# Attention's values as one group of 1,024 columns behind the gated heads, and GLA begun two column groups sooner

## The chip, the cores and the metric

The kernel runs on one core of a Trainium2 chip. The metric is the device time of one launch in microseconds. Each engine takes its instructions in order: TensorE (PE, with its weight loads apart as PEld), VectorE (DVE), ScalarE (ACT), GpSimd (POOL) and SyncE (SP), whose queue issues most of the DMA transfers. Engines wait for one another by semaphores.

## The reference

One layer of a decoder: an RMS norm, one projection to nine groups of columns, differential softmax attention (8 heads) and gated linear attention (GLA, 4 heads) side by side on the same input, both gated, and an output projection with a norm and a residual.

```python
def hybrid_layer(x, layer_idx, pre_g, post_g, w_in, w_gk_up, b_gk,
                 lq1, lk1, lq2, lk2, subln_g, gla_g, w_out):
    h = rms_norm(x, pre_g)
    z = jnp.einsum('bsd,de->bse', h, w_in)
    qa, ka, va, ga, qb, kb, vb, gb, gk_low = split_columns(z)
    lam = exp(sum(lq1 * lk1)) - exp(sum(lq2 * lk2)) + lam_init
    # softmax(q1 k1^T) v - lam softmax(q2 k2^T) v, causal, per head of 128 columns of va
    oa = diff_attention(qa, ka, va, lam)
    oa = rms_norm(oa, subln_g) * (1.0 - lam_init)
    oa = oa * silu(ga)
    log_a = log_sigmoid(gk_low @ w_gk_up + b_gk) / 16.0
    # S_t = diag(exp(log_a_t)) S_{t-1} + k_t^T v_t ; o_t = q_t S_t, in chunks
    ob = gla_chunked(qb, kb, vb, log_a)
    ob = rms_norm(ob, gla_g) * silu(gb)
    y = jnp.einsum('bse,ed->bsd', concatenate([oa, ob], -1), w_out)
    return x + rms_norm(y, post_g)
```

S and D_MODEL are 1024; va, the values of attention, has 1,024 columns (8 heads of 128). All is fp32.

## The kernel before

**Number format.** Each fp32 factor is split in a high part, cast by ACT, and a low part, its difference, taken by DVE; a product is three matmuls (high·high, high·low, low·high).

**Products.** The projection h·w_in is done for column groups, called pairs here (`pairs`, L168): VB, KA, QA, QB, KB, GB, VA, GA, each group 256 columns. For every group the 2x2 block product of h (rows in two halves, inner dimension in two halves) is made by seven products instead of eight, with sums of blocks; `LEFT` (L320) says which sum of h's blocks a product n = 1..7 takes. (VA0,5) is product 5 of the values' group that begins at head 0. b11, b12, b21, b22 are the blocks of the weights: the first digit is the half of the rows, the second the half of the columns. Products 1 and 2 take single blocks, 5, 6 and 7 differences that DVE makes in place in the loaded tiles, and their results are summed from banks of PSUM: a bank of 512 columns named x, y or z; s, s1, s2 and s3 are copies of partial sums that ACT makes.

**Two shapes.** For all groups but VA and VB the weights (128x128) are the stationary factor and 512 rows of h move; a product is 12 matmuls of 128x512. VA and VB need the result with rows on partitions, so a block of h is stationary and 256 columns of weights move: two groups of 256 columns go together ("wide"), they share the weights of a product, and each product of a group is 24 matmuls of 128x256. VA is done as two such couples, VA0 with VA2 and VA4 with VA6, one for each half of the heads: 28 products.

**The order.** The list `order` holds the products, (group, n), one after the other; product 3 of a group is placed behind product 2 (or 5, 6) of the next one. `go` (L598) runs down that list: it prepares weights four products ahead (`prepare`, then `make_weights`: load, subtract, cast, low part), calls `step` for the product and then, through `fill`, one section of GLA. A scheduler keeps the order of the matmuls and sets that of the other engines' instructions. Weights of a product go through a ring of five tiles of 128x1024 (`NRING`, tag "ring"), loaded weights through four tiles of 512 KB (tag "raw").

**GLA beside it.** `gla` (L771 and following) is cut into sections by `yield`: 11 sections a half, 8 halves, 88 sections. A half loads its inputs, does pa and pk, the kv states, gpo (its output, copied by ACT to the tile go), the squares, gms (their sum by a matmul), and then norms and gates go, splits it, and stores high parts (from the tile gg) and low parts (from go) to mixe. Its tiles are those that attention will need later, one buffer each in the pool kp: q0, k0, q1, k1, ks0, ks1; go is in ks0; gan, the squares sqs and their split sq_hl, which the gms matmuls read, share k1. GLA begins when the order stands at (12, 5), the group GB2, and its 88 sections, one a product, end beside the gated heads, at GA6.

**What comes around.** `decay` (L682 and following) makes the decays of GLA heads, which the taking of QB and KB needs; `wo_step` prepares pieces of the output's weights. `take_values` (L396) adds two banks into c, splits it, and stores it in v_d, from where attention loads it. Attention itself follows the last products, those of KA6 and QA6.

Of the kernel before, what the change touches and what calls it, by code (L numbers as in the profile page):

```python
# [14 lines left out]
P = 128  # L15
# [4 lines left out]
HB = 4  # L20
# [11 lines left out]
def hymba_kernel(  # L32
# [58 lines left out]
    v_d = [tc.dram_tile([2, P, NT, P], F32, name=f"v{h}_d") for h in range(DA_HEADS)]  # L91
# [78 lines left out]
    pairs += [("KA", 0, KA), ("QA", 0, QA), ("QB", 0, QB), ("KB", 0, KB)]  # L170
    pairs += [("GB", g, GB + 256 * g) for g in range(2)]
    pairs += [("QB", 2, QB + 256), ("KB", 2, KB + 256)]
    pairs += [("GB", g, GB + 256 * g) for g in range(2, 4)]
    for h in (0, 4):
        pairs += [("VA", h, VA + h * P), ("VA", h + 2, VA + h * P + 256)]
        pairs += [(n, h + 2, c + h * P + 256) for n, c in (("KA", KA), ("QA", QA)) if not h]
        pairs += [(n, 4, c + 512) for n, c in (("KA", KA), ("QA", QA)) if h]
    pairs += [("GA", g, GA + g * P) for g in range(0, DA_HEADS, 2)]
    pairs += [("KA", 6, KA + 768), ("QA", 6, QA + 768)]

    def wide(p):
        return pairs[p][0] in ("VA", "VB")
# [3 lines left out]
    def load_raw(p, halves=(0, 1)):  # L186
        if p >= len(pairs):
            return
        c0 = pairs[p][2]
        for kh in halves:  # L190
            if kh not in raws.setdefault(p, {}):
                r = ap.tile([P, HB, 256], F32, tag="raw", name="w_raw", bufs=4)
                rows = slice(kh * 512, kh * 512 + 512)
                sp.dma_start(r, w_in[0, rows, c0 : c0 + 256].rearrange("(k p) c -> p k c", p=P))
                raws[p][kh] = r

    EARLY = 5
# [4 lines left out]
    for p in range(y):  # L204
        if wide(p) and p % 2:
            groups[-1].append(p)
        else:
            groups.append([p])
    for prev, group in zip([[]] + groups, groups):
        for n in (1, 2, 5, 6, 4, 7):  # L210
            if (group[0], n) not in order[:n_early]:
                order += [(p, n) for p in group]

            if n == (7 - len(group) if group[0] < EARLY else 2):
                order += [(p, 3) for p in prev]
# [4 lines left out]
    order += [(y, 1), (y, 2), (y - 1, 3), (y, 5), (z, 1), (z, 2), (z, 5), (y, 6), (z, 6), (y, 4)]  # L220
# [29 lines left out]
    def fetch_raw(p, n, i):  # L250

        if not wide(p):
            load_raw(p)
            if i >= n_early:
                load_raw(p + 1)
        elif p >= 4 or p == 0:
            load_raw(p)
            if p and n == 1:
                load_raw(p + 1)

            if n == 4:
                load_raw(p + 2, (0,))
                if p == 0:
                    load_raw(3, (0,))
            elif n == 7:
                if p == 0:
                    load_raw(3, (1,))
                else:
                    load_raw(p + 2, (1,))
        else:  # L270
            if n == 5:
                load_raw(2, (1,))
            elif n == 4:
                load_raw(4, (0,))
            elif n == 7:
                load_raw(4, (1,))

    def make_weights(i):
        p, n = order[i]
        if wide(p) and p % 2:  # L280
            ws[i] = ws_wide[p - 1, n]
            return
# [63 lines left out]

    decs = {}
# [48 lines left out]
    def take_values(p, half, unit, p0, p1):  # L396

        kind, n, _ = pairs[p - p % 2]
        tiles = slice(half * 4 + p % 2 * 2, half * 4 + p % 2 * 2 + 2)
        p0, p1 = (t.rearrange("p (n u c) -> p u n c", u=2, c=P) for t in (p0, p1))  # L400
        if kind == "VB":
            st = t_st("gv_st").rearrange("p (u n c) -> p u n c", u=2, c=P)
            dve.tensor_tensor(st, p0, p1, ALU.add)
            for u in range(2):
                sp.dma_start(gv_d[n + unit][u, :, tiles, :], st[:, u])
        else:
            c, hi = t_c("c"), t_st("v_hi", F32R)
            c, hi, lo = (
                t.rearrange("p (u n c) -> p u n c", u=2, c=P) for t in (c, hi, c.bitcast(F32R))
            )  # L410
            dve.tensor_tensor(c, p0, p1, ALU.add)
            act.copy(hi, c)
            dve.tensor_tensor(lo, c, fp(hi), ALU.subtract)
            for t, src in enumerate((hi, lo)):
                for u in range(2):
                    sp.dma_start(v_d[n + 2 * unit + u][t, :, tiles, :], fp(src[:, u]))

    sums = {}

    def step(i):  # L420

        p, n = order[i]
        kind, m, _ = pairs[p]
# [175 lines left out]
    def go(n):  # L599
        for _ in range(n):  # L600
# [137 lines left out]
    go(order.index((8, 2)) - made[0])  # L738
    go(2)
    decay(2)  # L740
    go(7)
# [148 lines left out]
    go(order.index((12, 5)) - made[0])  # L890
# [99 lines left out]
    def load_v(h):  # L990
        v = [smp.tile([P, NT, P], F32R, tag="v", name=f"v{t}", bufs=4) for t in range(2)]
        for t in range(2):

            with tc.issue_after(qk_load[0]) if h else nullcontext():
                ins = sp.dma_start(fp(v[t]), v_d[h][t])
# [535 lines left out]
```

## Time and profile before

| what | us |
|---|---|
| time, three runs | 978.72, 978.31, 978.85 (median 978.72) |
| the profiled execution's own time | 978.49 |
| its span | 976.7 |
| PE busy | 956.6 |
| DVE busy | 735.4 |
| ACT busy | 602.1 |
| products of VA in the trace | from 308.8 on |
| last gms matmuls of GLA | 569.7 |

The profile is of one execution. Its span is the time in which the engines' instructions lie, and the difference to the execution's own time lies before and behind them. A row of a group of instructions gives the line, the engine, the operation, the output and input tiles and their shape, then how many there are, their busy time and the mean of one in ns, and the idle time ahead of them with what ended it. A row of the timeline gives the start, the duration and the count of instructions run together. Since PE's matmuls are pipelined, the duration of a group reaches into the next; the distance from start to start is what a group takes of PE's time.

### The profile page before, as it was taken

Reading aid. Unit: us, or ns where it says so; the run is one execution under the profiler, and the core shown is the slowest. Engines: PE = TensorE matmul, PEld = TensorE weight load, DVE = VectorE, ACT = ScalarE, POOL = GpSimd, SP = SyncE. Lnnn points to the kernel's source line nnn. Section 1 sums busy time; section 2 is a strip of 40 time slices with the busy share of each in tenths; the row PEclk is TensorE's granted clock in tenths of the full one; section 3 lists DMA queues with packets and bytes.
Section 4 is the critical chain, followed back from the end, with each engine's and each line's share of the span. In section 5 each row is a group of like instructions: output and inputs, shape, how many; then the busy total and the mean of one; then the engine's idle time right before and its main releaser. Section 6 shows DMA issues by size and latency. Waiting matters only on the chain.

```text
span 976.7 us, 15689 instructions
## 1 busy us (share of the span) xinstructions
PE 956.6 (98%) x5282; PEld 828.3 (85%) x5282; DVE 735.4 (75%) x1452; ACT 602.1 (62%) x1164; POOL 193.8 (20%) x253
## 2 busy tenths in 40 slices
PE   6999999999999999999999999999999999999997
PEld 5998988888889998999888888878888888888785
DVE  6887597798775668676786776487888888898554
ACT  8642455487357446545566765366776687787773
POOL 4300000111121111100321102121322222443321
PEclk9999999999999999999999999999999999999999
DMA  9442446656675859986988766987747769994777
GB/s 355 142 117 86 138 136 204 227 177 236 229 258 166 269 164 328 285 266 205 285 283 251 250 194 199 395 267 271 220 147 238 245 199 366 323 296 105 151 208 149
DMA packets 146513, 220.45 MB, mean 226 GB/s; under 512 B 17104, under 2 KB 83664, under 8 KB 146336
## 3 DMA queue, kind: packets, MB, share of 16 engines
q1 hardware_dynamic: 132496, 178.80, 57.5%
q0 software_dynamic: 13936, 40.64, 14.2%
q8 instruction: 42, 0.69, 0.3%
q14 instruction: 39, 0.32, 0.1%
HBM read 133.93 MB, written 88.60 MB: 228 GB/s over the span
## 4 chain that ended last, share of the span: by engine, by line
PE 93%; DVE 3%; ACT 2%; DMA 1%; issue 1%; POOL 0%; DVEq 0%; SPq 0%; ACTq 0%; POOLq 0%
PE x L117 23%; PE y L117 15%; PE z L117 15%; PE ypart L117 13%; PE sc L117 7%; PE po L117 5%; PE yps L117 4%; PE wtr L120 3%; PE gpo L117 3%; PE kv L117 1%; PE gkl_ps L117 1%; PE pa L117 1%; DMA v_d<-c 1%; PE xT L120 0%; ACT junk L491 0%
## 5 line engine op out<-in xcount | busy, mean ns | idle before, releaser
L315 ACT CAST w<-w_raw 128x512 fp32r<-128x512 f32 (+1 forms) x164 | 112.3, 688 | 107.2 <-PE y L117 50.0
L316 DVE TENSOR_TENSOR w<-w_raw,w 128x512 fp32r<-128x512 f32 (+1 forms) x164 | 126.6, 773 | 57.0 <-ACT w L315 48.8
L1054 ACT ACTIVATE p<-p,stt 128x896 f32<-128x896 f32 (+7 forms) x128 | 99.3, 777 | 36.2 <-DVE stt L1044 33.1
L427 ACT COPY s<-x 128x512 f32<-128x512 f32 x84 | 49.0, 583 | 91.9 <-PE x L117 91.5
L296 DVE TENSOR_TENSOR w_raw<-w_raw 128x512 f32<-128x512 f32 (+1 forms) x96 | 75.8, 790 | 21.2 <-DMA w_raw<-in_w_in_dram 19.7
L588 POOL DMA_DIRECT2D wo_d<-wo_hi x32 | 17.6, 550 | 349.7 <-ACT wo_hi L584 349.7
L1044 DVE CUSTOM_DVE_ANT_0 p<-sc,maskt 128x512 f32<-128x512 f32 (+3 forms) x128 | 74.3, 585 | 15.6 <-PE sc L117 14.3
L1060 POOL TENSOR_SCALAR p<-p,stt,lam 128x1024 f32<-128x1024 f32 (+3 forms) x64 | 56.2, 879 | 146.0 <-DVE stt L1059 144.3
L117 PE MATMUL y<-h_hi,w 128*128 128x512 f32 x320 | 79.9, 392 | 0.0
L117 PE MATMUL x<-s_hi,w 128*128 128x512 f32 x320 | 79.8, 391 | 0.0
L117 PE MATMUL ypart<-wo_hi,m_hi 128*128 128x512 f32 x192 | 79.6, 414 | 0.1
L117 PE MATMUL z<-s_hi,w 128*128 128x512 f32 x320 | 79.6, 391 | 0.0
L117 PE MATMUL ypart<-wo_hi,m_lo 128*128 128x512 f32 x192 | 75.5, 393 | 0.0
L117 PE MATMUL ypart<-wo_lo,m_hi 128*128 128x512 f32 x192 | 75.4, 393 | 0.0
L117 PEld LDWEIGHTS x<-s_hi,w 128*128 128x128 f32 x320 | 59.8, 188 | 12.3
L117 PEld LDWEIGHTS y<-h_hi,w 128*128 128x128 f32 x320 | 59.8, 188 | 12.3
L117 PE MATMUL sc<-k,q 128*128 128x512 f32 (+1 forms) x192 | 69.0, 363 | 1.2 <-DVE stt L1044 1.2
L117 PEld LDWEIGHTS z<-s_hi,w 128*128 128x128 f32 x320 | 59.5, 188 | 12.0
L117 PE MATMUL sc<-ks,q 128*128 128x512 f32 (+1 forms) x192 | 66.1, 347 | 0.0
L1102 ACT CAST wt_hi<-wtr 128x512 fp32r<-128x512 f32 (+1 forms) x80 | 42.7, 534 | 25.6 <-PE wtr L120 24.8
L1103 DVE TENSOR_TENSOR wt_lo<-wtr,wt_hi 128x512 fp32r<-128x512 f32 (+1 forms) x80 | 50.5, 632 | 7.1 <-ACT wt_hi L1102 6.7
L1063 DVE SCALAR_TENSOR_TENSOR p<-p,stt,p 128x1024 f32<-128x1024 f32 (+3 forms) x64 | 52.1, 814 | 4.5 <-POOL p L1060 4.1
(231 smaller groups left out, 2295.4 us busy)
## 6 DMA issues: line engine op xcount, KB each, us to landing
w_raw<-in_w_in_dram SPq DMA_DIRECT2D x56, 512.0 KB, 5.0
wo_d<-wo_hi POOLq DMA_DIRECT2D x32, 256.0 KB, 3.0
q<-q_d SPq DMA_DIRECT2D x32, 256.0 KB, 4.9
k<-k_d SPq DMA_DIRECT2D x32, 256.0 KB, 5.7
ks<-k_d SPq DMA_DIRECT2D x64, 128.0 KB, 6.1
v<-v_d SPq DMA_DIRECT2D x16, 512.0 KB, 6.6
wo_raw<-in_w_out_dram POOLq DMA_DIRECT2D x31, 256.0 KB, 4.9
wo_d<-gqd POOLq DMA_DIRECT2D x20, 256.0 KB, 4.7
```

The costliest lines, as they stand in the source:

```text
L117: tc.keep_in_program_order(pe.matmul(*a, **k))
L120: tc.keep_in_program_order(pe.transpose(dst, src, ident))
L296: dve.tensor_tensor(dst, a, b, ALU.subtract)
L315: act.copy(w[0], src)
L316: dve.tensor_tensor(w[1], src, fp(w[0]), ALU.subtract)
L427: act.copy(b[k], ps)
L1044: ins = dve.tensor_tensor_reduce(p[:, a:e], sc[:, : e - a], maskt[:, NZ + P - (e - a) :] if last else maskt[:, : e - a], 1.0, 3e38 if i == ...
L1054: act.activation(p[:, :n], p[:, :n], AF.Exp, bias=st[:, m : m + 1], scale=-1.0, accum_out=st[:, 2 + m : 3 + m],)
L1060: pool.tensor_scalar(p1[:, :n], p1[:, :n], st[:, 5:6], lam, ALU.mult, ALU.mult)
L1063: dve.scalar_tensor_tensor(p0[:, :n], p0[:, :n], st[:, 4:5], p1[:, :n], ALU.mult, ALU.subtract)
L1102: act.copy(hi[:, :n], pt[:, :n])
L1103: dve.tensor_tensor(lo[:, :n], pt[:, :n], fp(hi[:, :n]), ALU.subtract)
```

## The change

**The values.** The groups VA0+VA2 and VA4+VA6 become one group of 1,024 columns in two entries VA0 and VA2 (`VALS`), four row tiles in all, two to an entry. It stands behind GA6 and ahead of KA6 and QA6. The weight blocks are now 512 columns wide (b11 is rows 0 to 511, columns 0 to 511 of VA), each loaded as two tiles of 512 KB: b11 and b21 in the "raw" tiles, b12 in q0 and k0, b22 in k1 and ks0. `value_weights` makes two high and two low tiles of a product, four of the ring's five. `multiply_values` does 24 matmuls of 128x512 a product, into two banks; there are 14 products. The order of the parts is high·high, h's low part, weights' low part. `take_heads` does one row tile at a time and stores 256 KB a piece; the layout of v_d is turned to fit.

**The others.** QA0 goes from its place behind KA0 to one behind GB3; QB, KB and GB follow KA0 at once, in the order QB0, KB0, GB0, QB2, KB2, GB1, GB2, GB3. The decays are placed to fit. GLA begins at (9, 3) + 1, while GB1 is done, fifteen products earlier in the list, and runs two sections behind each product of the values. Its last sections now stand beside the values' first products. The pieces of the output's weights are prepared from KA0 on and not beside the values.

On PE, where the values begin before (VA0 and VA2, product 1; x, y, z are banks, h_hi and h_lo the parts of an activation block, w the weights; pa, pk belong to GLA's next half):

```order
L117 MATMUL gms<-sq_hl,ones 128x512 x2
L117 MATMUL x<-w,h_hi 128x256 x16
L117 MATMUL x<-w,h_lo 128x256 x8
...
L117 MATMUL pa<-kq 128x128 x4
L120 MATMUL pk<-ident,kq 128x128 x4
L117 MATMUL y<-w,h_hi 128x256 x16
```

On PE, at the end of GLA after the change, from the first product of VA2 to the third step behind gms, (VA0,6):

```order
L117 MATMUL x<-w,h_hi 128x512 x8
L117 MATMUL x<-w,h_lo 128x512 x8
...
L117 MATMUL y<-w,h_hi 128x512 x8
L117 MATMUL y<-w,h_lo 128x512 x8
...
L117 MATMUL gms<-sq_hl,ones 128x512 x2
...
L117 MATMUL z<-w,s_hi 128x512 x8
L117 MATMUL z<-w,s_lo 128x512 x8
L117 MATMUL z<-w,s_hi 128x512 x16
...
L117 MATMUL x<-w,s_hi 128x512 x8
```

Twice as many columns move a matmul, half as many matmuls are there, and GLA's last gms stands inside the values' second product, (VA0,2) before it and (VA2,2) behind it.

On SP, the last half of GLA before the change (mixe<-gg and mixe<-go are the stores of the high and low parts; g_d those of the attention gates; q1, k1, ks1, ks0 are loaded for attention):

```order
L861 DMA mixe_130<-gg_5626 128x4x128
L377 DMA g5_d_114<-c_5904 128x512
L861 DMA mixe_130<-gg_5626 128x4x128
L861 DMA mixe_130<-go_5655 128x4x128
L377 DMA g4_d_113<-c_5912 128x512
L861 DMA mixe_130<-go_5655 128x4x128
L194 DMA w_raw_6023<-in_w_in_dram 128x4x256
L883 DMA ks1_6248<-k0_d_93 64x512 x3
```

And after it (v_raw_5197 and v_raw_5199 are the two halves of b22, v0_d the stores of v, go_5007 the last half's output):

```order
L214 DMA v_raw_5197<-in_w_in_dram 128x2x512
L466 DMA v0_d_101<-v_hi_5268 128x4x128
...
L466 DMA v0_d_101<-c_5274 128x4x128
L944 DMA mixe_124<-gg_4989 128x4x128 x2
L466 DMA v0_d_101<-v_hi_5338 128x4x128
L944 DMA mixe_124<-go_5007 128x4x128
L466 DMA v0_d_101<-v_hi_5345 128x4x128
L944 DMA mixe_124<-go_5007 128x4x128
L466 DMA v0_d_101<-c_5337 128x4x128
...
L214 DMA v_raw_5199<-in_w_in_dram 128x2x512
```

The stores of go now have a load behind them, v_raw_5199, that is written to their own source tile ks0 and waits for them.

On DVE, after the change, from the norm of the last half's output on (w_5207 and w_5209 are low parts of product 5's weights, w_5307 one of product 6's; v_raw_4788 and v_raw_4790 are the halves of b11, v_raw_5107 one of b12, c_5337 a sum of values):

```order
L936 SCALAR_TENSOR_TENSOR go_5007<-go_5007,gla_g_80,r_5284 128x512 x2
L302 TENSOR_TENSOR v_raw_5107<-v_raw_5197,v_raw_5107 128x1024
L939 TENSOR_TENSOR go_5007<-go_5007,gg_4989 128x512
L309 TENSOR_TENSOR w_5207<-v_raw_4788,w_5203 128x1024
...
L309 TENSOR_TENSOR w_5209<-v_raw_4790,w_5205 128x1024
L462 TENSOR_TENSOR c_5337<-y_5311,s_5237 128x512
...
L942 TENSOR_TENSOR go_5007<-go_5007,gg_4989 128x512
L302 TENSOR_TENSOR v_raw_4788<-v_raw_5197,v_raw_4788 128x1024
...
L464 TENSOR_TENSOR c_5337<-c_5337,v_hi_5338 128x512
...
L302 TENSOR_TENSOR v_raw_4790<-v_raw_5199,v_raw_4790 128x1024
...
L309 TENSOR_TENSOR w_5307<-v_raw_4788,w_5303 128x1024
```

The subtraction that needs the first half of b22 stands ahead of both products of go with the gates (L939) and of its low parts (L942), and the one that needs the second half ahead of product 6's low weights.

The diff, cut to its core:

```diff
     pairs = [("VB", g, VB + 256 * g) for g in range(4)]
-    pairs += [("KA", 0, KA), ("QA", 0, QA), ("QB", 0, QB), ("KB", 0, KB)]
-    pairs += [("GB", g, GB + 256 * g) for g in range(2)]
+    pairs += [("KA", 0, KA), ("QB", 0, QB), ("KB", 0, KB), ("GB", 0, GB)]
     pairs += [("QB", 2, QB + 256), ("KB", 2, KB + 256)]
-    pairs += [("GB", g, GB + 256 * g) for g in range(2, 4)]
-    for h in (0, 4):
-        pairs += [("VA", h, VA + h * P), ("VA", h + 2, VA + h * P + 256)]
-        pairs += [(n, h + 2, c + h * P + 256) for n, c in (("KA", KA), ("QA", QA)) if not h]
-        pairs += [(n, 4, c + 512) for n, c in (("KA", KA), ("QA", QA)) if h]
+    pairs += [("GB", g, GB + 256 * g) for g in range(1, 4)]
+    pairs += [("QA", 0, QA)]
+    pairs += [(n, h, c + h * P) for h in (2, 4) for n, c in (("KA", KA), ("QA", QA))]
     pairs += [("GA", g, GA + g * P) for g in range(0, DA_HEADS, 2)]
+    VALS = (len(pairs), len(pairs) + 1)
+    pairs += [("VA", t, VA) for t in (0, 2)]
     pairs += [("KA", 6, KA + 768), ("QA", 6, QA + 768)]
...
+    def load_values(name):
+
+        if name not in value_raws:
+            c0 = VA + (name[2] == "2") * 512
+            r0 = (name[1] == "2") * 512
+            value_raws[name] = []
+            for i, tag in enumerate({"b12": ("q0", "k0"), "b22": ("k1", "ks0")}.get(name, ("raw",) * 2)):
+                if tag == "raw":
+                    r = ap.tile([P, 2, 512], F32, tag=tag, name="v_raw", bufs=4)
+                else:
+                    r = kp.tile([P, 2, 512], F32, tag=tag, name="v_raw")
+                rows = slice(r0 + i * 256, r0 + i * 256 + 256)
+                sp.dma_start(r, w_in[0, rows, c0 : c0 + 512].rearrange("(k p) c -> p k c", p=P))
+                value_raws[name].append(r)
...
+    va, vb = VALS
+    order += [(va, 1), (va - 1, 3), (vb, 1)] + [(p, n) for n in (2, 5, 6, 7, 4, 3) for p in VALS]
...
+    def value_weights(n):
+
+        for name in {1: ("b11", "b21"), 2: ("b12",), 5: ("b22",), 3: ()}.get(n, ()):
+            load_values(name)
...
+        src = {1: b11, 2: b21, 5: b11, 6: b11, 7: b12, 4: b21, 3: b22}[n]
+        sums = {5: ((b11, b12),), 6: ((b11, b22), (b21, b21)), 7: ((b12, b22),)}.get(n, ())
+        for dst, a in sums:
+            for i in range(2):
+                dve.tensor_tensor(dst[i], a[i], (b12 if n == 7 else b11)[i], ALU.subtract)
+        his, los = [], []
+        for i in range(2):
+            his.append(ap.tile([P, 2, 512], F32R, tag="ring", name="w", bufs=NRING))
+            act.copy(his[i], src[i])
+        for i in range(2):
+            los.append(ap.tile([P, 2, 512], F32R, tag="ring", name="w", bufs=NRING))
+            dve.tensor_tensor(los[i], src[i], fp(his[i]), ALU.subtract)
+        return his, los
...
+        for j, (a, b) in enumerate(((0, hi), (0, lo), (1, hi))):
+            for k in range(HB):
+                for u, ps in enumerate(pss):
+                    c = ((p - VALS[0]) * 2 + u) * P
+                    mm(
+                        ps, at(b, k)[:, c : c + P], w[a][k // 2][:, k % 2, :],
...
+    def take_heads(tile, unit, p0, p1):
+
+        c, hi = t_c("c"), t_st("v_hi", F32R)
+        lo = c.bitcast(F32R)
+        dve.tensor_tensor(c, p0, p1, ALU.add)
+        act.copy(hi, c)
+        dve.tensor_tensor(lo, c, fp(hi), ALU.subtract)
+        for t, src in enumerate((hi, lo)):
+            sp.dma_start(
+                v_d[unit][:, t, :, tile, :].rearrange("u p c -> p u c"),
+                fp(src).rearrange("p (u c) -> p u c", c=P),
             )
...
-            if order[i][0] > EARLY and not (wide(order[i][0]) and order[i][0] % 2):
+            if order[i][0] >= EARLY and order[i][0] not in VALS:
                 wo_step(order[i][1])
-            if fill and next(fill[0], 0) == 0:
-                fill.pop(0)
+            for _ in range(2 if order[i][0] in VALS else 1):
+                if fill and next(fill[0], 0) == 0:
+                    fill.pop(0)
...
-    go(order.index((8, 2)) - made[0])
-    go(2)
+    go(order.index((6, 3)) + 1 - made[0])
     decay(2)
-    go(7)
+    go(4)
     decay(3)
...
-    go(order.index((12, 5)) - made[0])
+    go(order.index((9, 3)) + 1 - made[0])
     fill.append(chain(*(gla(g) for g in range(GLA_HEADS))))
```

More of the change, by code (lines that the diff above doesn't have):

```diff
@@ L203, in hymba_kernel @@
     groups = []
-    for p in range(y):
+    for p in range(VALS[0]):
         if wide(p) and p % 2:
@@ L396, in take_values @@
     def take_values(p, half, unit, p0, p1):
-        kind, n, _ = pairs[p - p % 2]
+        n = pairs[p - p % 2][1]
         tiles = slice(half * 4 + p % 2 * 2, half * 4 + p % 2 * 2 + 2)
         p0, p1 = (t.rearrange("p (n u c) -> p u n c", u=2, c=P) for t in (p0, p1))
[L401 to L409, printed above, removed]
-            )
[L411 to L416, printed above, removed]
@@ new lines, in hymba_kernel, with step_values @@
+    sums = {}
+    def step_values(i):
+        p, n = order[i]
+        state = sums.setdefault(p, [{}, {}])
+        name = {1: "x", 2: "y", 5: "z", 6: "x", 4: "y", 7: "x", 3: "z"}[n]
+        if n in (1, 2, 5, 4):
+            for b in state:
+                b[name], b["i" + name] = take_bank([P, 512], name)
+        multiply_values(i, [b[name] for b in state], n not in (6, 7, 3))
+        if n == 7:
+            s3 = kp.tile([P, 2, 512], F32, tag="ks1" if p == VALS[0] else "q1", name="s3")
+        for u, b in enumerate(state):
+            t = (p - VALS[0]) * 2 + u
+            ps = b[name]
+            if n in (1, 6):
+                k = "s1" if n == 1 else "s2"
+                b[k] = t2k("s", 4, "s")
+                act.copy(b[k], ps)
+            elif n == 7:
+                b["s3"] = s3[:, u]
+                act.copy(b["s3"], ps)
+                free.append(b["ix"])
+                take_heads(4 + t, 1, b["z"], b["s3"])
+            elif n != 5:
+                half, unit, k = {2: (0, 0, "s1"), 4: (1, 0, "s3"), 3: (0, 1, "s2")}[n]
+                take_heads(half * 4 + t, unit, ps, b[k])
+                free.append(b["i" + name])
```

50 lines of the change are left out of this document (33 added, 17 removed).

## The prediction

> **What bounds the kernel now.** The page's head was read first, then TensorE's list of waits, then its timeline.
>
> ```profile
> span 976.7 us, 15689 instructions
> PE 956.6 (98%) x5282; PEld 828.3 (85%) x5282; DVE 735.4 (75%) x1452; ACT 602.1 (62%) x1164; POOL 193.8 (20%) x253
> PEclk9999999999999999999999999999999999999999
> PE 93%; DVE 3%; ACT 2%; DMA 1%; issue 1%; POOL 0%; DVEq 0%; SPq 0%; ACTq 0%; POOLq 0%
> ...
> PE xT L120 <- DVE x L482: 8.8, 4, 7.4
> ...
> PE kv L117 <- DVE c L411: 0.2, 1, 0.2
> ```
>
> TensorE (PE) is busy for 956.6 of 976.7 us, the chain that ended last is PE for 93%, and the clock is full throughout. The waits (us in total, times, longest; first and last of seven rows) begin with 8.8 us for the input at the start, and the only one that the values' projection appears in is 0.2 us. So a gain must come from fewer or denser matmuls, and any wait that is new on PE is added to the time whole. I sum against this execution's own 978.49 us; the median of the runs, 978.72, is 0.23 above it.
>
> **The gain: wider matmuls.** A product of the old shape is 24 matmuls of 128x256; one of the new is 24 of 128x512, a shape that the other projections already use, twelve to a product. PE's timeline (start, duration of the group) has both:
>
> ```profile
> 206.41 1.98 PE L117 MATMUL x<-h_hi,w 128*128 128x512 f32 x8
> 208.23 1.07 PE L117 MATMUL x<-h_lo,w 128*128 128x512 f32 x4
> 209.13 1.98 PE L117 MATMUL y<-h_hi,w 128*128 128x512 f32 x8
> ...
> 308.78 2.08 PE L117 MATMUL x<-w,h_hi 128*128 128x256 f32 x16
> 310.70 1.13 PE L117 MATMUL x<-w,h_lo 128*128 128x256 f32 x8
> 311.66 2.08 PE L117 MATMUL x<-w,h_hi 128*128 128x256 f32 x16
> ```
>
> Start to start, 24 narrow ones take 311.66 − 308.78 = 2.88 us (120 ns each) and 12 wide ones 209.13 − 206.41 = 2.72 us (227 ns each). Before there are 28 such products, 80.64 us; after, 14 of 24 wide ones, 14 × 5.44 = 76.16 us. That is −4.48 us, all of it on PE's path. The Trainium skill ("TensorE: Matmul & The Clock Gate", section "Back-to-back issue gap") gives an isolated matmul N/2.4 + 2.5 ns, by which two narrow ones lose only one such 2.5 ns to a wide one. By that, my estimate of the gain would be 336 × 2.5 ns = 0.84 us, and the whole sum 3.6 us worse; the trace's 13 ns a pair (2 × 120 − 227) differs, and the measurement decides.
>
> **What costs nothing.** Loads (eight of 512 KB), casts, low parts, subtractions and adds keep number and size. The stores of v keep their 8 MB in 32 pieces of 256 KB instead of 64 of 128 KB, and the queue's rows below have both sizes (4.4 or 5.8 us against 3.5 or 4.7 to landing); their c tiles have four buffers, so I take 0, and the 1.1 us between 4.7 and 5.8 is what a reuse would wait at most, on DVE. GLA's sections now lie beside the gated heads and the q/k pairs only. While a half ran beside the gated heads before, PE had no idle time and neither DVE nor ACT was full:
>
> ```profile
> 520.00:570.00 50.00, 50.00 (x255) 42.59 (x254) 36.06 (x57) 34.93 (x64) 5.64 (x9) 1.00 0.73 234
> ```
>
> (Window; busy PE, PEld, DVE, ACT, POOL; clock; DMA share; GB/s.) So the earlier start of GLA and the exchange of QA0 cost 0. The decays run with fewer steps behind them:
>
> ```profile
> 214.57 0.62 PE L117 MATMUL gk<-gkl,ku 128*128 128x512 f32 x2
> 235.23 1.05 ACT L712 ACTIVATE b<-b 128x1024 f32<-128x1024 f32 x1
> ```
>
> The last head's decay took 236.3 − 214.6 = 21.7 us from its first matmul, and its first user now comes seven products (7 × 2.72 = 19.0 us) behind: between 0 and 2.7 us. I take 0, because four matmul banks and the c tiles let PE run ahead of the taking of a product, and keep 2.7 for a rival.
>
> **The new wait: b22's second half.** The values' sums need whole 512-row blocks of the weights in tiles, so b12 and b22 are loaded into GLA's tiles. The last half of b22 goes into ks0, which is the tile of GLA's output go. Its load therefore waits until both stores of go's low part have landed; these stores wait for DVE, which makes the low parts; and DVE, in its order, first waits for b22's first half, which goes into k1, free only when the last gms matmuls are done. PE's third product behind gms's pair, (VA0,6), needs that last half after four matmuls. The rows for each link:
>
> ```profile
> w_raw<-in_w_in_dram SPq DMA_DIRECT2D x56, 512.0 KB, 5.0
> mixe<-gg SPq DMA_DIRECT2D x16, 256.0 KB, 4.4
> mixe<-go SPq DMA_DIRECT2D x16, 256.0 KB, 5.8
> v_d<-v_hi SPq DMA_DIRECT2D x32, 128.0 KB, 3.5
> v_d<-c SPq DMA_DIRECT2D x32, 128.0 KB, 4.7
> ...
> DMA to landing us min/median/max: 3.5/5.0/9.2
> ...
> DMA to landing us min/median/max: 2.2/5.5/8.5
> ```
>
> (The issues with their median us to landing, then the spreads of w_raw's and of mixe's transfers.)
>
> ```profile
> L316 DVE TENSOR_TENSOR w<-w_raw,w 128x1024 fp32r<-128x1024 f32 x26 | 32.0, 1235 | 7.8 <-PE x L117 4.9 <-issue 1.9 <-PE z L117 0.9
> L315 ACT CAST w<-w_raw 128x1024 fp32r<-128x1024 f32 x26 | 27.1, 1048 | 27.1 <-PE z L117 11.7 <-DVE w_raw L296 10.9 <-PE y L117 4.4
> L296 DVE TENSOR_TENSOR w_raw<-w_raw 128x1024 f32<-128x1024 f32 x16 | 20.5, 1280 | 15.6 <-DMA w_raw<-in_w_in_dram 15.5
> L372 ACT ACTIVATE g<-c 128x512 f32<-128x512 f32 x32 | 19.8, 630 | 4.9 <-DVE c L440 4.7
> L859 DVE TENSOR_TENSOR go<-go,gg 128x512 fp32r<-128x512 f32 x16 | 10.9, 698 | 1.2 <-ACT gg L857 1.1
> L856 DVE TENSOR_TENSOR go<-go,gg 128x512 f32<-128x512 f32 x16 | 10.7, 684 | 0.0
> L411 DVE TENSOR_TENSOR c<-y,s 128x512 f32<-128x512 f32 x8 | 5.5, 682 | 3.1 <-DMA v_d<-c 3.1
> ```
>
> The clock starts at the end of gms. First half of b22: 5.0. Then on DVE, in its new order: subtraction 1.28, two products with two weights' low parts between them 2 × 0.68 + 2 × 1.235, two adds 1.36, one low part of go 0.70, one subtraction 1.28, the other low part 0.70: 9.15, so 14.2. Store 5.8: 20.0. Load 5.0: 25.0. Subtraction 1.28 and cast 1.05: 27.3. PE, unstalled, does (VA2,2), (VA0,5), (VA2,5) in 3 × 5.44 = 16.32 and four matmuls more, 0.91: 17.2. The stall is 10.1 us, less the 0.1 by which the second small wait below has already delayed PE: 10.0. Ends: with both kinds of transfer at their shortest (3.5, 2.2, 3.5) 20.7 − 17.2 − 0.1 = 3.4; at their longest (9.2, 8.5, 9.2) 38.4 − 17.3 = 21.1. I take the medians because the queue has four stores of v and two of gate parts ahead of these, the traffic that the medians were made in. That DVE needs this long has a check in the last half of GLA before, where nothing of b22 stood between:
>
> ```profile
> 569.72 0.62 PE L117 MATMUL gms<-sq_hl,ones 128*128 128x512 f32 x2
> 574.02 1.28 DVE L856 TENSOR_TENSOR go<-go,gg 128x512 f32<-128x512 f32 x2
> 578.07 0.52 SPq L861 DMA_DIRECT2D mixe<-go  x1
> 579.32 0.41 SPq L861 DMA_DIRECT2D mixe<-go  x1
> ```
>
> Even there the last store of go left 9.6 us after gms began; 9.6 + 5.8 + 5.0 + 2.3 = 22.7 would still stall by 5.4. Nobody waited for those stores then.
>
> **Two small waits.** b12's second half waits in the same way for the last gpo matmuls; behind it on DVE stands the add that three ACT operations of a gate wait for, and behind two of those the cast of n=2's second weight. 5.0 + 1.28 + 0.68 + 3 × 0.63 + 1.05 = 9.9 us after gpo, where PE arrives after (GA6,3) 2.72, (VA2,1) 5.44 and 0.91 = 9.1: 0.8 us (0 to 4.9, by the load's 3.5 and 9.2). The low weights of n=5 stand on DVE behind b22's first half: 5.0 + 1.28 + 0.68 + 1.235 + 0.68 + 1.235 = 10.1 against 5.44 + 20 × 0.227 = 10.0 for its last weight: 0.1 us (0 to 4.3).
>
> **The clock behind the gap.** PE idles for long only at the start, the 8.8 us in four pieces of the list above; behind it stands:
>
> ```profile
> 13.63 4.24 PE L117 MATMUL x<-w,h_hi 128*128 128x256 f32 x16 [0.38 <-ACT h_hi L521]
> 17.67 1.79 PE L117 MATMUL x<-w,h_lo 128*128 128x256 f32 x8
> 19.29 1.91 PE L120 MATMUL xT<-ident,x 128*128 128x128 f32 x16
> ```
>
> The first 24 matmuls took 19.29 − 13.63 = 5.66 us, against 2.88 later: 2.8 us lost. I charge 2.8 behind a gap of 10.0 us, with 0 as the other end, since no gap of this length stands inside the kernel. The Trainium skill ("TensorE: Matmul & The Clock Gate", section "HAM oscillation — how this bites in real kernels") says that a wait above some 3.4 us puts TensorE back to half clock, with about 1.67 us throttled each time there. As an estimate from its half clock over a 3.4 us window the loss would be 1.7 us, and the sum 1.1 lower; the start's row agrees in kind and is larger.
>
> **The sum.** 978.49 − 4.48 + 0.8 + 0.1 + 10.0 + 2.8 = 987.7 us.
>
> **The rivals.**
> A is this forecast. B: the stall without the clock's loss, 984.9; for it, that the only cold start seen is also the program's first, against it that those matmuls ran at just half speed.
> C, on the other side: the transfers are fast behind gms, because GLA's own loads end there. With all three at their shortest, the small waits at 0 and a gap too short for the clock, 978.5 − 4.5 + 3.4 = 977.4; some 0.4 less if DVE's nine operations overlap as the two products of 1.28 us (not 1.37) in the row above do. It decides from where the load, the store and the second load together stay under 12 us instead of 15.8, with a stall of 6.2 and still the full clock: 980.2. To be faster by 0.2% the stall must be under 2.8, so the three together under 8.5, a little below the shortest of the rows (9.2). Against it, the window above shows 234 GB/s with the queue at 73%, and the transfers listed here come closer together than GLA's.
> D: the early decay costs its 2.7 us too: 990.4. Against it, PE shows no wait for the decay before.
> The change does what it says in all four: the order of the matmuls is fixed.
>
> **How the numbers follow.** A 0.62, B 0.15, C 0.15, D 0.08. A measurement of this kernel tells 0.2%, 2.0 us, from no change. C splits into 0.09 faster, for transfers and operations at or under the shortest rows, and 0.06 within; the low ends of A and B add 0.01 to faster and 0.03 to the middle: faster 0.10, same 0.09, slower 0.81. The range leaves out most of C and the longest transfers of A: 979 to 994, a stall of 5 us at the full clock and one of 16 with the loss. The forecast is 987.5, A's sum in round numbers.
>
> **What would show it.** PE's 14 wide products of 5.44 us; a PE wait of some 10 us ahead of (VA0,6), ending in ACT's cast, behind it DVE's subtraction, and behind that a load of 512 KB issued after two stores of go have landed; a dip in the clock row just there; less than a microsecond of waits at (VA0,2) and (VA0,5). If (VA0,6) starts within 3 us, the prediction is wrong in the stall; if a wait stands around the decays, in the early part.

## The result, and the profile after

The changed kernel takes 983.51 us (median; 981.42 to 988.07) against 978.72 before (977.89 to 979.0). The ratio is 1.0051, with a 95% interval of 1.0038 to 1.0064: it is slower, by about 5 us. The profiled execution took 983.51 us as well; its span is 981.8 us, 5.1 above that of before. The head of its page:

```profile
span 981.8 us, 14991 instructions
PE 954.9 (97%) x4946; PEld 812.4 (83%) x4946; DVE 734.3 (75%) x1452; ACT 602.6 (61%) x1164; POOL 187.7 (19%) x253
PE 83%; DMA 6%; issue 4%; DVE 4%; ACT 1%; POOL 1%; SPq 0%; DVEq 0%; POOLq 0%; ACTq 0%
```

PE is busy for less time than before, and is 83% of the chain that ended last instead of 93%; transfers are 6% of it now. PE's list of waits (in all, times, longest) names three that were not there, w L306, the longer of the two rows of s L510, and a small one in attention, p L1146:

```profile
PE x L117 <- ACT w L306: 3.8, 1, 3.8
PE x L117 <- ACT s L510: 2.5, 1, 2.5
...
PE wtr L120 <- DVE p L1146: 0.6, 1, 0.6
```

**At the values.** PE's timeline from GLA's last gms on:

```profile
530.24 0.62 PE L117 MATMUL gms<-sq_hl,ones 128*128 128x512 f32 x2
...
536.35 1.98 PE L117 MATMUL z<-w,s_hi 128*128 128x512 f32 x8
...
547.23 1.07 PE L117 MATMUL x<-w,s_hi 128*128 128x512 f32 x4
552.10 1.65 PE L117 MATMUL x<-w,s_hi 128*128 128x512 f32 x4 [3.80 <-ACT w L306]
553.54 3.16 PE L117 MATMUL x<-w,s_lo 128*128 128x512 f32 x8
556.55 3.81 PE L117 MATMUL x<-w,s_hi 128*128 128x512 f32 x16
```

(VA0,5) and (VA2,5) run from 536.35 to 547.23, 10.88 us, so a product is 5.44. (VA0,6) stops after four matmuls, exactly where its second high weight is needed. The four take 0.91 us at full speed, so they are through at 548.14, and PE goes on at 552.10: 3.96 us. The twelve matmuls from there to 556.55 take 4.45 us instead of 12 × 0.227 = 2.72: the clock costs another 1.73 us. The granted clock shows it (us; busy PE, PEld, DVE, ACT, POOL; clock; DMA share; GB/s; why the stretches are cut at these times is said in the last section):

```profile
549.24:552.65 3.41, 0.55 (x2) 0.49 (x3) 2.96 (x3) 1.65 (x2) 0.00 (x0) 1.00 0.00 1
552.65:556.06 3.41, 3.41 (x9) 2.63 (x8) 2.81 (x3) 0.35 (x1) 0.00 (x0) 0.50 0.15 29
```

The chain that ended last shows what PE waited for, in order of time:

```profile
542.45 0.61 DVE go L942
...
543.08 2.25 DMA mixe<-go
...
545.40 4.27 DMA v_raw<-in_w_in_dram
...
549.69 1.24 DVE v_raw L302
...
551.00 1.05 ACT w L306
```

**In the early part.** The second wait is ahead of (KB2,7), in the stretch whose order the change has altered. PE, then ACT and POOL, from the timeline:

```profile
222.81 1.07 PE L117 MATMUL y<-h_lo,w 128*128 128x512 f32 x4
226.38 2.11 PE L117 MATMUL x<-s_hi,w 128*128 128x512 f32 x8 [2.50 <-ACT s L510]
```

```profile
212.43 0.62 ACT L667 CAST wo_hi<-wo_raw 128x512 fp32r<-128x512 f32 x1
...
214.56 0.54 POOL L671 DMA_DIRECT2D wo_d<-wo_raw  x1 [0.68 <-DVE wo_raw L669]
...
219.43 0.55 POOL L679 DMA_DIRECT2D wo_raw<-in_w_out_dram  x1 [4.33 <-DMA wo_d<-wo_raw]
...
225.22 0.62 ACT L667 CAST wo_hi<-wo_raw 128x512 fp32r<-128x512 f32 x1 [6.12 <-DMA wo_raw<-in_w_out_dram]
225.75 0.58 ACT L510 COPY s<-x 128x512 f32<-128x512 f32 x1
```

One piece of the output's weights goes round here: cast on ACT, low part, store from its raw tile, load of the next piece into the same tile once that store has landed, next cast. That took 225.22 − 212.43 = 12.8 us. ACT stood 6.12 us at the second cast, and behind it in its order is the copy of product 6's sum, without which PE can't begin product 7 in the same bank. The same place in the kernel before:

```profile
247.90 0.62 ACT L584 CAST wo_hi<-wo_raw 128x512 fp32r<-128x512 f32 x1 [1.65 <-DMA wo_raw<-in_w_out_dram]
...
259.37 0.62 ACT L584 CAST wo_hi<-wo_raw 128x512 fp32r<-128x512 f32 x1 [2.67 <-DMA wo_raw<-in_w_out_dram]
259.89 0.58 ACT L427 COPY s<-x 128x512 f32<-128x512 f32 x1
...
261.27 1.98 PE L117 MATMUL x<-s_hi,w 128*128 128x512 f32 x8
```

There the round took 11.5 us, and the copy ended 0.8 us before PE came to product 7 (259.89 + 0.58 against 261.27). It was hidden, with 0.8 us to spare. Two windows, with the same columns as above, show the transfers around it, of before first:

```profile
244.00:256.00 12.00, 12.00 (x54) 9.93 (x54) 11.13 (x19) 3.98 (x7) 2.18 (x4) 1.00 0.67 221
```

```profile
214.00:226.00 12.00, 9.88 (x44) 7.86 (x42) 8.21 (x15) 2.12 (x5) 1.09 (x2) 1.00 0.89 301
```

The DMA engines are busier at this place than before, 0.89 against 0.67.

**The sum of the spans.** 976.7 − 4.48 (width) + 3.96 + 1.73 (at (VA0,6)) + 2.50 + 0.13 (at (KB2,7), the 2.11 against 1.98 behind it) gives 980.5. The rest lies where nothing was changed. The matmuls of the second decay start 0.5 us later (135.31 instead of 134.79), and that is there already when PE's first wait on s ends (43.82 against 43.27). It is scatter between executions: in the kernels below that are the same as the changed one up to there, that wait ends between 42.73 and 43.80. Another 0.6 us are in attention (from its first ypart matmul at 630.04 it took 346.7 before; from 634.54 it takes 347.3), which is the wait on p in the list.

### The profile page after: what moved, and what is told of

Same layout as the page of the kernel before. It is cut to its first block, busy times and chain, and to the rows that moved or that the text cites. A ratio compares the mean times of both kernels' runs of the same rounds, so it can differ in the third digit from the quotient of the medians.

```text
span 981.8 us, 14991 instructions
## 1 busy us (share of the span) xinstructions
PE 954.9 (97%) x4946; PEld 812.4 (83%) x4946; DVE 734.3 (75%) x1452; ACT 602.6 (61%) x1164; POOL 187.7 (19%) x253
## 4 chain that ended last, share of the span: by engine, by line
PE 83%; DMA 6%; issue 4%; DVE 4%; ACT 1%; POOL 1%; SPq 0%; DVEq 0%; POOLq 0%; ACTq 0%
PE x L117 20%; PE ypart L117 13%; PE y L117 12%; PE z L117 11%; PE sc L117 7%; PE po L117 5%; PE yps L117 4%; PE wtr L120 3%; PE gpo L117 3%; DMA wo_d<-wo_raw 3%; DMA wo_raw<-in_w_out_dram 2%; PE kv L117 1%; DMA w_raw<-in_w_in_dram 1%; PE gkl_ps L117 1%; PE pa L117 1%
## 5 line engine op out<-in xcount | busy, mean ns | idle before, releaser
L352 ACT CAST w<-w_raw 128x512 fp32r<-128x512 f32 (+1 forms) x150 | 98.0, 655 | 99.1 <-PE y L117 42.3
L353 DVE TENSOR_TENSOR w<-w_raw,w 128x512 fp32r<-128x512 f32 (+1 forms) x150 | 109.6, 732 | 40.2 <-ACT w L352 39.6
L510 ACT COPY s<-x 128x512 f32<-128x512 f32 x72 | 42.2, 586 | 71.3 <-PE x L117 71.0
L1127 DVE CUSTOM_DVE_ANT_0 p<-sc,maskt 128x512 f32<-128x512 f32 (+3 forms) x128 | 74.2, 585 | 14.3 <-PE sc L117 12.8
L333 DVE TENSOR_TENSOR w_raw<-w_raw 128x512 f32<-128x512 f32 (+1 forms) x88 | 65.6, 746 | 10.6 <-DMA w_raw<-in_w_in_dram 9.4
L1146 DVE SCALAR_TENSOR_TENSOR p<-p,stt,p 128x1024 f32<-128x1024 f32 (+3 forms) x64 | 52.1, 814 | 5.1 <-POOL p L1143 4.8
```

The costliest lines, as they stand in the source:

```text
L333: dve.tensor_tensor(dst, a, b, ALU.subtract)
L352: act.copy(w[0], src)
L353: dve.tensor_tensor(w[1], src, fp(w[0]), ALU.subtract)
L510: act.copy(b[k], ps)
L1127: ins = dve.tensor_tensor_reduce(p[:, a:e], sc[:, : e - a], maskt[:, NZ + P - (e - a) :] if last else maskt[:, : e - a], 1.0, 3e38 if i == ...
L1146: dve.scalar_tensor_tensor(p0[:, :n], p0[:, :n], st[:, 4:5], p1[:, :n], ALU.mult, ALU.subtract)
```

## The experiments

Times are medians, and ratios are to the kernel before, whose median was 978.20 us beside the first runs (the other tile, half the width, the early part alone, the low part in a c tile) and 978.26 us beside the others.

**Another tile for b22.** In the changed kernel, b22 no longer goes to the tile of go:

```diff
-{"b12": ("q0", "k0"), "b22": ("k1", "ks0")}
+{"b12": ("q0", "k0"), "b22": ("q1", "k1")}
-            s3 = kp.tile(..., tag="ks1" if p == VALS[0] else "q1", name="s3")
+            s3 = kp.tile(..., tag="ks1" if p == VALS[0] else "ks0", name="s3")
```

> The changed kernel with one thing moved: b22's first half goes to q1 (free once GLA's last gpo matmuls have read gqd) and its second half to k1, and the copies s3 of VA2 go to ks0 instead of q1. No load waits for the stores of go any more. If the chain over those stores made the wait ahead of (VA0,6) (4.0 us) and the clock's loss behind it (1.7 us), both vanish: 983.5 - 5.7 = 977.8 us, and 975.3 if the 2.5 us wait near 226 us does not come back. If the stall came from DVE's or the queue's load in general, another wait stands at (VA0,6) or (VA0,7), and the time stays above 981.

975.82 us; ratio 0.9975 (0.9963 to 0.9987). PE's timeline at the same place:

```profile
544.09 1.98 PE L117 MATMUL z<-w,s_hi 128*128 128x512 f32 x8
545.91 1.98 PE L117 MATMUL x<-w,s_hi 128*128 128x512 f32 x8
547.72 1.98 PE L117 MATMUL x<-w,s_lo 128*128 128x512 f32 x8
```

The wait is gone, and with it the clock's loss: (VA0,6) runs at 1.81 us per eight matmuls. PE's list has 1.8 us for the copies s in two waits, near 224 and 245 us, so the early wait has come back, smaller. The difference to the changed kernel is 7.7 us by the medians and 7.2 by the two profiled executions (983.51 against 976.29). Of these, 5.7 us lie between the last gms matmul and attention's first ypart matmul (104.1 us against 98.4), the size of the wait and the clock's loss; 0.9 us lie ahead of the second decay, where the two kernels are the same, and 0.6 elsewhere. The changed kernel's executions spread more widely: its slowest, 988.07 us, has a granted clock of 0.992 against 0.997 in the profiled one, and 0.005 × 986 = 4.9 us is about what it is longer by.

**Half the width.** As the last kernel, with each 128x512 matmul of the values made as two of 128x256:

```diff
+                    for t in range(2):
+                        mm(ps[:, t * 256 : t * 256 + 256], at(b, k)[:, c : c + P],
+                           w[a][k // 2][:, k % 2, t * 256 : t * 256 + 256], ...)
```

> As the kernel with the other tile, but each matmul of the values, 128x512, is made as two of 128x256 with the same stationary block. If the width is worth what the rows of before say (120 against 227 ns), this one is 4.5 us slower than the kernel with the other tile. If the width is hidden or the weights' loads set the pace, no difference; by the isolated gap of 2.5 ns a matmul, 0.8 us.

980.72 us; ratio 1.0026 (1.0017 to 1.0036), 4.9 us above the kernel with the other tile. In its timeline sixteen narrow matmuls take 537.96 − 536.04 = 1.92 us:

```profile
536.04 2.08 PE L117 MATMUL z<-w,s_hi 128*128 128x256 f32 x16
537.96 2.08 PE L117 MATMUL z<-w,s_lo 128*128 128x256 f32 x16
```

Against 1.81 for eight wide ones that is 0.11 us in each of 14 × 3 groups, 4.6 us. From GLA's first gms matmul to attention's first ypart matmul, the stretch that holds the values, the profiled execution takes 362.4 us against 358.0 with the other tile alone, 4.4 more. The gain that was worked out is real and whole.

**A longer gap.** The changed kernel, b22 in its old tiles, with three more stores behind each store of go's low part in the last half (they write the low part to a place that nothing reads):

```diff
+                if g == GLA_HEADS - 1 and half == 1:
+                    for e in range(3):
+                        sp.dma_start(extra[3 * t + e], o[:, t])
```

> The changed kernel with six more stores of go's low part in the last half of GLA (three behind each of the two, to a place that nothing reads), so b22's second half waits for them too: the gap ahead of (VA0,6) grows from 4.0 us to some 7 to 11 us. If the clock's loss behind a gap is one fixed window, the first matmuls behind it lose 1.7 us as in the changed kernel, and the time is 983.5 plus the growth of the gap alone, 986.5 to 990.5. If the loss grows with the gap, as the prediction took it from the start of the program, it is 2.8 us.

987.37 us; ratio 1.0093 (1.0073 to 1.0113).

```profile
545.19 1.07 PE L118 MATMUL x<-w,s_hi 128*128 128x512 f32 x4
553.77 2.08 PE L118 MATMUL x<-w,s_hi 128*128 128x512 f32 x4 [7.51 <-ACT w L307]
555.64 2.67 PE L118 MATMUL x<-w,s_lo 128*128 128x512 f32 x8
558.15 3.80 PE L118 MATMUL x<-w,s_hi 128*128 128x512 f32 x16
```

The gap is 553.77 − 545.19 − 0.91 = 7.67 us, so the stores of go do set when the load starts. The twelve matmuls behind it take 558.15 − 553.77 = 4.38 us, 1.66 too many: as much as behind 3.96 us. The granted clock:

```profile
550.26:553.67 3.41, 0.00 (x0) 0.00 (x0) 2.31 (x3) 1.00 (x2) 0.00 (x0) 0.50 0.10 40
553.67:557.09 3.42, 3.32 (x8) 2.65 (x9) 3.42 (x4) 0.99 (x2) 0.00 (x0) 0.50 0.03 2
```

The clock is at half for twice as long as in the changed kernel, but in the first half of that PE stands anyhow. What is lost is half of the time that PE works at half clock, 3.32 us here, so 1.66 us. So the loss did not grow with the gap.

**The early part alone.** The kernel before with the other order of QA0, QB, KB and GB, the decays and the start of GLA, as in the change; values as before:

```diff
-    pairs += [("KA", 0, KA), ("QA", 0, QA), ("QB", 0, QB), ("KB", 0, KB)]
+    pairs += [("KA", 0, KA), ("QB", 0, QB), ("KB", 0, KB), ("GB", 0, GB)]
...
+    pairs += [("QA", 0, QA)]
...
-    go(order.index((12, 5)) - made[0])
+    go(order.index((9, 3)) + 1 - made[0])
```

> The kernel before with only the first half of the change: QA0 behind GB3, QB, KB and GB directly behind KA0, the decays placed to fit, GLA two pairs sooner. The values stay where and as they were, 256 columns a matmul in two couples, and the pieces of the output's weights begin one pair later than in the changed kernel, as before. If the early part costs nothing: 978.7, within 0.2%. If the 2.5 us wait belongs to the early part: 981.2. If it is worth something by itself: under 976.8.

982.07 us; ratio 1.0037 (1.0024 to 1.0051). So the part that was taken as free costs 3.9 us by itself. Its timeline has the same wait at the same product:

```profile
225.01 3.28 PE L117 MATMUL x<-s_hi,w 128*128 128x512 f32 x8 [2.31 <-ACT s L427]
...
229.46 1.98 PE L117 MATMUL x<-h_hi,w 128*128 128x512 f32 x8
```

Here the clock fell, too: the product took 229.46 − 225.01 = 4.45 us instead of 2.72, another 1.73 us, behind a gap of 2.31 us:

```profile
222.24:225.65 3.41, 1.10 (x6) 0.58 (x5) 1.40 (x3) 1.79 (x4) 0.70 (x2) 1.00 0.88 305
225.65:229.06 3.41, 3.41 (x10) 2.63 (x9) 2.54 (x4) 0.34 (x1) 0.38 (x1) 0.50 0.74 287
```

In the changed kernel a gap of 2.50 us at the same product cost 0.13, and the granted clock stayed full.

**The early part with one turn of the pieces left out.** As the last one, but no piece is cast or loaded at (KB2,1) and (KB2,2), so the piece that was loaded before them is cast only at (KB2,6); the pieces end one turn later:

```diff
-            if order[i][0] > EARLY and not (wide(...) ...):
+            if order[i][0] > EARLY and order[i] not in ((9, 1), (9, 2)) and not (wide(...) ...):
```

> The kernel before with the early part of the change alone, as in the run of that name, but with the same one turn of the pieces left out at (KB2,1) and (KB2,2). If that one piece is all that the early part costs, it comes back to the kernel before: 978.2, within 0.2%. If the early part costs elsewhere too, it stays above 980.2.

979.42 us; ratio 1.0011 (1.0003 to 1.002). The wait at (KB2,7) is gone, and 2.7 of the 3.9 us with it. A cast still stands ahead of the copy of product 6's sum:

```profile
210.82 0.55 POOL L596 DMA_DIRECT2D wo_raw<-in_w_out_dram  x1 [4.73 <-DMA wo_d<-wo_raw]
...
217.96 0.62 ACT L584 CAST wo_hi<-wo_raw 128x512 fp32r<-128x512 f32 x1 [2.57 <-DMA gq_d<-gqd]
220.21 0.59 ACT L427 COPY s<-x 128x512 f32<-128x512 f32 x1 [1.11 <-PE x L117]
```

But its piece was sent for at 210.82, 7.1 us ahead of the cast and not 4.4 as in the run above (219.43 and 223.85), and ACT waits 2.57 us there, for another transfer, instead of 5.93. The copy then waits for PE, and not PE for the copy. The remaining 1.2 us are neither nothing nor above the 980.2 that was set for a second cost. In PE's list stand three small waits that the kernel before doesn't have; they may be it:

```profile
PE gpo L117 <- DVE gu L809: 0.6, 1, 0.6
PE sc L117 <- DMA ks<-k_d: 0.6, 1, 0.6
...
PE pa L117 <- DMA kq<-gq_d: 0.3, 1, 0.3
```

**The same turn left out beside the other tile.**

```diff
-            if order[i][0] >= EARLY and order[i][0] not in VALS:
+            if order[i][0] >= EARLY and order[i][0] not in VALS and order[i] not in ((9, 1), (9, 2)):
```

> The kernel with the other tile, with one turn of the pieces of the output's weights left out: at the products (KB2,1) and (KB2,2), so no piece is open at (KB2,6), and the pieces end one turn later. If the wait of PE ahead of (KB2,7) near 225 us comes from the piece's load standing in ACT's order ahead of the copy of product 6's sum, it goes: 1 to 2.5 us faster than the kernel with the other tile (975.8), so 973.5 to 974.8. If ACT or the transfers are late there anyhow, for the decay's work or GLA's loads, the wait stays at about 1 to 2 us with another releaser, and the time is 975.8.

973.89 us; ratio 0.9953 (0.9941 to 0.9965), the fastest of all. A piece is still open at (KB2,6), other than expected; as in the run before, it was loaded earlier, and its cast doesn't hold up the copy. In its profile the wait at (KB2,7) is gone, and so is the one near 245 us; near them is left a wait of 0.3 us for GLA's first load. It is 1.9 us below the kernel with the other tile alone, whose two waits come to 1.8 us. The profiled execution is the slowest of its five, 975.68 us, only 0.6 below the other's. It has two waits that the other has not: 0.91 us at the program's start, and 0.85 us at 166.64, where ACT again stands at a piece's cast (4.47 us, for the piece's load) ahead of a copy. Without them it would be at the median.

**The decay sooner.** The kernel with the other tile, and the last decay begun two products sooner:

```diff
     decay(2)
-    go(4)
+    go(2)
     decay(3)
```

> The kernel with the other tile, with the last head's decay begun two products sooner. If the decay's work on ACT and DVE beside (KB2,1) is what makes the piece's cast late, and so the wait ahead of (KB2,7), the wait goes: 1 to 2.5 us faster, 973.5 to 974.8. If the transfers' landings alone make it, it stays: 975.8. If the decays then stand in each other's way, another wait appears ahead of (QB2,1)'s taking: slower.

978.66 us; ratio 1.0003 (0.9992 to 1.0013): not faster, 2.8 us slower than without it. The wait at (KB2,7) is still there, 1.31 us, and the timeline has the piece's round still too long:

```profile
212.82 0.62 ACT L667 CAST wo_hi<-wo_raw 128x512 fp32r<-128x512 f32 x1 [4.14 <-DMA wo_raw<-in_w_out_dram]
...
219.42 0.55 POOL L679 DMA_DIRECT2D wo_raw<-in_w_out_dram  x1 [4.42 <-DMA wo_d<-wo_raw]
224.01 0.62 ACT L667 CAST wo_hi<-wo_raw 128x512 fp32r<-128x512 f32 x1 [4.88 <-DMA wo_raw<-in_w_out_dram]
```

The first cast was late because its own load was, and not because the decay's work stood ahead of it. So it is the round of the piece, 11.2 us here, against the four products of 2.72 us that lie between two casts. Why the kernel is slower by as much as 2.8 us its profile doesn't show: the profiled execution, with a span of 975.5 us, is one of its quick ones, and takes as long as the kernel with the other tile from the second decay to attention (493.2 against 493.1 us). Seven of its twelve executions have a granted clock of 0.997 or 0.996, the profiled one 0.998, so in those the clock fell somewhere; but the other five, with 975.31 to 978.69 us, are slower in the middle too. The cause stays open.

**The low part in a c tile.** As the kernel with the other tile, but the next piece's load need not wait for a store to land:

```diff
-            lo = (spare[0][:, 1] if spare else raw).bitcast(F32R)
+            lo = spare[0][:, 1].bitcast(F32R) if spare else t_c("wo_lo", F32R)
```

> As the kernel with the other tile, but until GLA's tile is there the low part of a piece of the output's weights goes to one of the four c tiles instead of back into the piece's own raw tile, so the next piece's load no longer waits for that store to land. If the 2.5 us wait near 226 us comes from that load coming late to ACT, it goes: 2.5 us under the kernel with the other tile where that one has it, else no difference. If the c tiles then run short, a new wait on them appears and it is slower.

976.01 us; ratio 0.998 (0.9971 to 0.9989), no difference to the kernel with the other tile. The wait on the copy is gone from its profile, and the next thing is late, the load of GLA's first half:

```profile
238.69 1.13 PE L117 MATMUL pa<-kq 128*128 128x128 f32 x8 [1.45 <-DMA kq<-gq_d]
```

So by the medians a freed load of a piece gained nothing, and a piece left out did. The profiled executions don't tell the two apart: from the second decay to attention's first ypart matmul both take 492.4 us, against 493.1 with the other tile alone. Whether it matters that a piece left out takes its transfers from beside GLA's first ones was not tried apart.

## Why the prediction was right in sign and too large

It gave 987.5 us, 979 to 994, and slower at 0.81. The time is 983.5, so the sign and the range held, and 8.8 us of loss were forecast where there are 4.8. The sizes behind the total are others than those forecast:

| term of the sum | forecast | profile after |
|---|---|---|
| width, 28 to 14 products | −4.48 | −4.48, and 4.9 by the narrow kernel |
| two small waits | 0.8 + 0.1 | 0 |
| stall at (VA0,6) | 10.0 | 3.96 |
| clock behind it | 2.8 | 1.73 |
| early part | 0 | 2.50 + 0.13 |
| where nothing was changed | 0 | 0.5 + 0.6 |

**Luck has a part in it.** In the profiled execution the width, the stall and the clock come to −4.48 + 3.96 + 1.73 = 1.2 us, inside the 2.0 us that the prediction took for no change. The 2.6 us of the early part, which it had put at nothing, and the 1.1 us where nothing was changed carried the time clear of that; terms too large and a term left out made up for one another. By the medians the sign is safer: moving the tile alone is worth 7.7 us against a gain of 4.5 to 4.9.

**The gain** was right. The other price given for it, one isolated gap of 2.5 ns saved for each pair of matmuls, 0.84 us, is refuted for this shape by the narrow kernel.

**The stall** was right in its place and in each of its links, and mis-sized in the transfers. From the end of gms, 530.70, to 552.06 it is 21.4 us instead of 27.3. The store took 2.25 us where the median 5.8 was put in: 3.55 us of the 5.9. The low end of the range (2.2) was the better choice for it. The two loads took 4.1 (with 0.3 to their issue) and 4.3 instead of 5.0 each, 1.6 us together; DVE's operations, ten and not nine as the prediction says further down, 8.2 instead of 9.15 us. The prediction's check against the last half of GLA before counts 9.6 us from the start of gms, but PE's 17.2 from its end, some 0.5 us later; the stall of 5.4 us there should be 4.9. The reason given for the medians, the traffic of the same stores, did not hold for the loads: the eight of the values have a median of 3.9 us. The stores of go still have one of 5.5 us after the change, so that this one landed in 2.25 could not be read from a group's row.

```profile
v_raw<-in_w_in_dram SPq DMA_DIRECT2D x8, 512.0 KB, 3.9
```

The same row answers for the small waits: with the shorter loads there are none, as their lower ends said.

**The clock's loss** was taken from the start of the program, 2.8 us, and is 1.7. The estimate by the Trainium skill ("TensorE: Matmul & The Clock Gate", section "HAM oscillation — how this bites in real kernels"), 1.7 us, agrees with 1.73 behind 3.96 us and 1.66 behind 7.67. The start was not another kind of loss but a longer stretch: in the trace of before the clock's first step to full is at 19.18, so PE worked from 13.63 on for 5.55 us before it, and half of that is the 2.8 us. The rival without a loss, B, falls.

**The step that failed** is "So the earlier start of GLA and the exchange of QA0 cost 0". It rested on a window in which PE had no idle time, 520 to 570 us, and that is not the stretch whose order was changed. The wait there is of the size of rival D, 2.5 against its 2.7 us, but not by its mechanism: an earlier decay doesn't remove it, and leaving out one turn of a piece does. What hung on ACT's order there, the copy of a product's sum behind a cast that waits for a transfer, could be read in the trace of before, with its 0.8 us to spare.

**C**, the faster rival, decided at a stall of 6.2 us with the full clock; the three transfers took 10.6 us together, under the 12 that it asked for. By that alone the time would have been nearly the same as before, and the clock and the early part made it slower.

## What to carry to other kernels

A tile lent to a load is free only when the last store out of it has landed: before lending, list each candidate's last reader, and give the one with a store to the use that comes last. When an order is changed, look in the trace of before for the waits in front of shared in-order engines that were hidden just there, and for how much was to spare; a stretch without idle time elsewhere says nothing of it. With spare time under a microsecond, two programs with the same work differ by as much as a good edit gains: here a gain of 4.5 us was worth −4.8 us with both waits, and 4.4 us once one tile and one turn of a piece were moved.

## What was not expected of the hardware

Whether the clock falls is not set by the gap's length alone. The loss was 1.73 us behind a gap of 2.31, 1.73 behind 3.96 and 1.66 behind 7.67 us, but 0.13 us behind 2.50. The rule that a wait above some 3.4 us is needed (the Trainium skill, "TensorE: Matmul & The Clock Gate", section "HAM oscillation — how this bites in real kernels") doesn't hold for the 2.31 us here.

The traces' own record of the granted clock shows what decides. In each of the ten traces the clock changes only at whole multiples of 3.413 us after its first step to full. In the changed kernel that first step is at 20.17; the fall at 552.65 is 532.48 us later, 156 × 3.413, and the return at 556.06 is one more. The windows above are cut at these times, and so are these two around the early gap of the changed kernel:

```profile
221.56:224.97 3.41, 2.32 (x11) 1.58 (x9) 0.52 (x1) 0.00 (x0) 0.00 (x0) 1.00 1.03 367
224.97:228.38 3.41, 2.00 (x9) 1.67 (x10) 2.16 (x4) 2.14 (x4) 1.08 (x2) 1.00 0.85 319
```

The gap of 2.50 us falls on both sides of 224.97: PE is idle for 1.09 us in one stretch and 1.41 in the next, and the clock stays full. The gap of 2.31 us with the early part alone lies within one stretch (3.41 − 1.10 = 2.31), and the next one runs at half clock; so it is behind the 2.86 us of one stretch ahead of (VA0,6). Inside the kernels the clock fell behind every stretch with 2.31 us or more of idle PE and behind none with 1.52 us or less; where between these the limit lies no wait inside a kernel shows. At the very end of the programs it fell behind 2.08 us (966.61 to 970.02, the kernel with the other tile) and not behind 1.85 us (969.99 to 973.41, the early part with one turn left out). The loss is half of what PE works before the stretch at half clock ends, so 1.7 us for a whole one. Part 1 of the same page of the Trainium skill says that the clock's activity window runs freely. The traces agree: the onset is a matter of where the gap falls. The first step to full lies between 17.4 and 20.2 us in them, and so the same wait can cost one execution 1.7 us and another nothing.

The transfers of one shape spread widely: a store of go of 256 KB landed within 2.25 us at the values, where the median of its group is 5.8 before. A chain of three transfers can't be priced by medians without a look at what is in the queues just then.
